# Final rows of an MLA / RG-LRU trunk normalised in place, with half of each row squared and weighted one product ahead, and one operand of the last projection split on VectorE

## Chip, cores and metric

The kernel runs on one core of one Trainium2 chip. The metric is the device time of one execution in microseconds (us); several executions are timed and their median is taken. One further execution is recorded by the hardware profiler, and every time of an instruction below is from that one.

## What is computed

A trunk of two layers, a latent-attention layer and an RG-LRU layer, over 1024 tokens and 16 leading meta tokens of width 1024, all in float32. The change lies in the end of the second layer and in the final norm:

```python
def rmsnorm(x, g):
    xf = x.astype(jnp.float32)
    y = xf * lax.rsqrt(jnp.mean(xf * xf, axis=-1, keepdims=True) + RMS_EPS)
    return (y * g.astype(jnp.float32)).astype(x.dtype)

# rglru_mixer: ... hs from the recurrence, gate from the input projection
    y = hs.astype(h.dtype) * jax.nn.silu(gate)
    return y @ w_out                       # (1040 x 1024) @ (1024 x 1024)

# after the two layers, h being the residual stream
    h = h + rglru_mixer(...)
    h = rmsnorm(h, final_norm_g)
    return h[:, N_META:]                   # the 1024 real tokens
```

## The kernel before

**Precision.** A float32 operand is split into a high part (a copy rounded to the matmul's type, `hi_of` at L80, ScalarE) and a low part (operand minus high part, `lo_of` at L83, VectorE). A product is three matmuls (`mm3`, L85 to L88: high x high, high x low, low x high), all accumulated in one PSUM bank.

**The last projection.** `Y` holds the gated mixer output, channels on partitions: `Y[:, ct, token]` for eight channel tiles `ct`. The projection of the 1024 real tokens is done as a 2 x 2 block scheme with seven block products of 512 x 512 x 512 in place of eight. `yq(cq, tq)` (L888) is a view of one block of `Y`; `a11, a12, a21, a22` (L974) are its four blocks, and sums and differences of them are made in place (L976, L993, L1007, L1008). The weight blocks and their sums come through `w_raw` / `w_load` (L864 to L874; a load with `add` accumulates by DMA on the GpSimd queue) and are split by `w_split` (L876) into buffers of the pools `wpg` and `pw1`, two of a kind. The operand from `Y` is split by `y_split` (L892): ScalarE copies (L893), VectorE subtracts (L894). `yc` (L935) does so for a whole block of 2048 elements a partition, into the tags `ych` and `ycl` of the pool `bo`, two buffers each. That pool opens at L926, when the pools of the layer's normalised input (`x2`) are closed: its buffers lie where that input lay, so they come free when the last gate product has read it.

**Products.** `product` (L896) runs four banks of 128 tokens, 12 matmuls of 512 columns in each. In program order the products are w1 (into banks `b2`), w7 (onto `b2`), w2 (into `b1`), w6 (onto `b2`), w5 (into `b3`), w3 (onto `b3`), w4 (onto `b2`). Between them `upd` (L946) adds or subtracts a bank into a half (`LEFT` or `RIGHT`, 512 columns) of a row tile `hr[i]`, 128 tokens x 1024, which was loaded from `hscr` at L932; a bank that a later product accumulates onto must have been read first. `hr[0..3]` are the first 512 tokens, `hr[4..7]` the last. The left half of `hr[0..3]` is final after w2's update, the right half of `hr[4..7]` after w3 begins, the right half of `hr[0..3]` after w3, the left half of `hr[4..7]` after w4.

**The final norm.** `square(i, half)` (L955) squares a half on ScalarE with its sum accumulated; the squares are thrown into an output tile `ot`, of which there are two (L958). `finish(i)` (L963) adds the two sums, takes a square root on ScalarE (L132) and refines it with four one-column VectorE instructions (L133 to L140), then writes `ot = hr * r * g_f` in two halves on VectorE (L970), each sent out by the SP queue (L971). `hr[0..3]` are finished after w3, `hr[4..7]` after w4.

**Order of the work.** The kernel is written on a tile framework that is told to plan with a timeline (L1084): when it is compiled, a planner with its own costs merges the program's instructions into one fixed order per engine, the earlier in the program the sooner among what it takes to be ready. On the chip each engine's queue is worked off in that order, and each instruction waits for its own operands. The ScalarE splits of the first operand `y1` (L913 to L918) already go into buffers of the recurrence (pool `bw`, tags `up`, `uh`, `ul`), ahead of the last gate product `b_gate(KT - 1, g7)`; the second operand, `y7` (L977, the block difference `a21 - a11`), goes through `yc`.

Of the kernel before, what the change touches and what calls it, by code (L numbers as in the profile page):

```python
# [8 lines left out]
F32 = mybir.dt.float32  # L9
# [8 lines left out]
P = 128  # L18
# [44 lines left out]
def trunk(ctx, tc, x, meta, a_norm_g, a_w_in, a_q_g, a_kv_g, a_w_uq, a_w_ukv, a_w_out,  # L63
# [832 lines left out]
    def product(banks, w, ys, first):  # L896
        for i in range(TI):
# [10 lines left out]
    w_load(ra, 0, 1)  # L908
    b_gate(KT - 1, g7)
# [3 lines left out]
    y1 = []  # L913
    for j in range(2):
        yh = pbw.tile([P, 4, 256], F32R, name=f"y1h{j}", tag=("up", "uh")[j], bufs=2)
        yl = pbw.tile([P, 4, 256], F32R, name=f"y1l{j}", tag=("up", "ul")[j], bufs=2)
        y_split(yq(0, 0, 256 * j, 256), yh, yl, -1)
        y1.append((yh, yl))  # L918
    w_load(ra, 1, 1, True)
    b2 = [ps_m(f"b2_{i}") for i in range(TI)]  # L920
    product(b2, w1, lambda i: (*y1[i // 2], (i % 2) * P), True)
    st_bw.close()
# [4 lines left out]
    st_fo, pfo = open_pool("fo", bufs=2, side="right")  # L927
# [25 lines left out]
    fms, junks = {}, {}  # L953

    def square(i, half):  # L955
        if i not in fms:
            fms[i] = sml.tile([P, 2], F32, name=f"fms{i}", tag="ms2", bufs=2 * TI)
            junks[i] = pfo.tile([P, D], F32, name=f"ot{i}", tag="ot", bufs=2)  # L958
        c = slice(half * 512, half * 512 + 512)
        nc.scalar.activation(junks[i][:, c], hr[i][:, c], AF.Square, scale=1.0 / 32.0,  # L960
                             accum_out=fms[i][:, half:half + 1])

    def finish(i):  # L963
        ot = junks[i]
        mt = sml.tile([P, 1], F32, name=f"fmt{i}", tag="ms")
        nc.vector.tensor_tensor(mt, fms[i][:, 0:1], fms[i][:, 1:2], ALU.add)
        r, _ = rms_r(mt, P, 1, f"f{i}")
        for half in range(2):
            c = slice(half * 512, (half + 1) * 512)
            nc.vector.scalar_tensor_tensor(ot[:, c], hr[i][:, c], r, g_f[:, c], ALU.mult, ALU.mult)  # L970
            nc.sync.dma_start(out[i * P:(i + 1) * P, c], ot[:, c])  # L971


    a11, a12, a21, a22 = yq(0, 0), yq(1, 0), yq(0, 1), yq(1, 1)  # L974
    w7 = w_split(ra, wpg, "wt3")
    nc.vector.tensor_tensor(a21, a21, a11, ALU.subtract)  # L976
    y7 = yc(a21, "s3")  # L977
# [110 lines left out]
```

## Time and profile before

| | us |
|---|---|
| median of 3 runs | 932.37 (928.75, 932.37, 932.37) |
| the profiled execution | 928.06 |
| its span, first to last instruction | 926.3 |
| TensorE busy in it | 888.9 (96%) |
| VectorE busy | 584.7 (63%) |
| ScalarE busy | 466.3 (50%) |

The profiled execution is a single one and lies just below the fastest of the three timed ones. The span leaves out the 1.8 us that lie around the first and last instruction. Mean granted TensorE clock is 0.994 of full speed (2.4 GHz). Engine names: PE is TensorE's matmul, PEld its weight load, DVE VectorE, ACT ScalarE, POOL GpSimd, SP the queue that issues most DMAs (SPq). Times of single instructions are from the start of the span.

### The profile page before, as it was taken

To read this page: it belongs to the slowest core of one execution; us is meant where nothing else is said; L and a number is where in the kernel's file an instruction comes from. 1 tells how busy PE (TensorE), PEld (TensorE's weight loads), DVE (VectorE), ACT (ScalarE), POOL (GpSimd) and SP (SyncE) were. 2 spreads that over 40 slices of the span, in tenths; PEclk is the share of its full clock that TensorE was granted. 3 is DMA by queue.
4 is the path that set the end of the run, shared out by engine and by line. 5 is a ranking of instruction groups with operands and counts; after the bars stand their busy time and mean duration, and the time that the engine had idled before them with its cause. 6 is when DMAs were issued, how large, how long until landed. Compare 5 with 4: busy or idle time off the path is not lost.

```text
span 926.3 us, 13669 instructions
## 1 busy us (share of the span) xinstructions
PE 888.9 (96%) x5279; PEld 816.0 (88%) x5279; DVE 584.7 (63%) x1206; ACT 466.3 (50%) x932; POOL 43.6 (5%) x46
## 2 busy tenths in 40 slices
PE   7999999999999999999999999999999999998993
PEld 5999999999999999999987778799989899886882
DVE  6666424416777677677675258764663947849986
ACT  6554322225664665665655146435648455582433
POOL 3000000000000000000000000000110201203100
PEclk9999999999999999999999999999999999999997
DMA  7123245221110010010032353241111111537613
GB/s 271 47 67 82 80 112 156 71 79 31 37 35 17 16 62 16 17 62 16 8 108 75 127 161 105 82 81 46 45 47 46 46 46 46 139 90 235 128 46 136
DMA packets 71169, 72.25 MB, mean 78 GB/s; under 512 B 15056, under 2 KB 52688, under 8 KB 71104
## 3 DMA queue, kind: packets, MB, share of 16 engines
q1 hardware_dynamic: 68928, 67.19, 23.4%
q0 software_dynamic: 2176, 4.19, 2.7%
q8 instruction: 41, 0.67, 0.3%
q14 instruction: 24, 0.20, 0.1%
HBM read 58.65 MB, written 12.71 MB: 77 GB/s over the span
## 4 chain that ended last, share of the span: by engine, by line
PE 89%; DVE 4%; ACT 3%; DMA 3%; issue 1%; SPq 1%; DVEq 0%; ACTq 0%
PE pt L536 4%; PE pu L88 3%; PE ga L86 3%; PE pu L86 3%; PE ga L87 3%; PE ga L88 3%; PE pu L87 3%; PE pg L87 3%; PE pg L88 3%; PE pg L86 3%; PE ao L86 3%; PE ao L88 3%; PE ao L87 3%; PE s L491 2%; PE o L88 2%; PE o L87 2%
## 5 line engine op out<-in xcount | busy, mean ns | idle before, releaser
L509 ACT ACTIVATE p<-s,m 116x116 f32<-116x116 f32 (+4 forms) x80 | 55.3, 693 | 42.8 <-PE pt L536 15.2
L80 ACT ACTIVATE pth<-pt 116x348 fp32r<-116x348 f32 (+5 forms) x152 | 57.5, 396 | 29.3 <-PE pt L536 25.7
L83 DVE TENSOR_TENSOR ptl<-pt,pth 116x348 fp32r<-116x348 f32 (+5 forms) x152 | 64.0, 437 | 10.3 <-ACT pth L80 9.6
L88 PE MATMUL pu<-x2h,l_wu 128*128 128x348 f32 (+1 forms) x192 | 61.5, 321 | 0.4 <-DVE l_wu L83 0.4
L88 PE MATMUL ga<-xth,l_wg 128*128 128x348 f32 (+1 forms) x192 | 61.7, 321 | 0.0
L87 PE MATMUL pu<-x2l,h_wu 128*128 128x348 f32 (+1 forms) x192 | 61.7, 321 | 0.0
L86 PE MATMUL pu<-x2h,h_wu 128*128 128x348 f32 (+1 forms) x192 | 61.7, 322 | 0.0
L87 PE MATMUL ga<-xtl,h_wg 128*128 128x348 f32 (+1 forms) x192 | 61.6, 321 | 0.0
L86 PE MATMUL ga<-xth,h_wg 128*128 128x348 f32 (+1 forms) x192 | 61.6, 321 | 0.0
L501 DVE CUSTOM_DVE_ANT_0 s<-s,maskt 116x116 f32<-116x116 f32 (+8 forms) x72 | 49.4, 686 | 17.6 <-PE s L495 17.6
L536 PE MATMUL pt<-ident,p 116*116 116x116 f32 (+1 forms) x360 | 54.5, 263 | 2.3 <-DVE ptl L83 1.8
L86 PE MATMUL ao<-wah,yh_a 128*128 128x512 f32 x128 | 50.5, 396 | 1.6 <-ACT yh_a L80 1.0
L87 PE MATMUL pg<-x2l,h_wbg 128*128 128x512 f32 x128 | 50.6, 396 | 0.0
L88 PE MATMUL pg<-x2h,l_wbg 128*128 128x512 f32 x128 | 50.3, 393 | 0.0
L88 PE MATMUL ao<-wah,yl_a 128*128 128x512 f32 x128 | 50.3, 394 | 0.0
L86 PE MATMUL pg<-x2h,h_wbg 128*128 128x512 f32 x128 | 50.2, 393 | 0.0
L87 PE MATMUL ao<-wal,yh_a 128*128 128x512 f32 x128 | 49.9, 391 | 0.0
L491 PE MATMUL s<-kh,qh 128*116 128x348 f32 (+7 forms) x120 | 42.1, 351 | 6.7 <-ACT p L509 6.7
L536 PEld LDWEIGHTS pt<-ident,p 116*116 116x116 f32 (+1 forms) x360 | 41.4, 135 | 6.0 <-DVE ptl L83 2.5
L87 PE MATMUL o<-ptl,v 116*128 116x348 f32 (+1 forms) x144 | 45.1, 313 | 0.0
L88 PE MATMUL o<-pth,v 116*128 116x348 f32 (+1 forms) x144 | 43.9, 305 | 0.0
L86 PE MATMUL o<-pth,v 116*128 116x348 f32 (+1 forms) x144 | 43.0, 298 | 0.0
(316 smaller groups left out, 2645.0 us busy)
## 6 DMA issues: line engine op xcount, KB each, us to landing
wg<-in_a_w_in SPq DMA_DIRECT2D x8, 512.0 KB, 3.9
wa<-in_a_w_out SPq DMA_DIRECT2D x8, 512.0 KB, 3.5
wu<-in_b_w_in SPq DMA_DIRECT2D x8, 512.0 KB, 4.0
wbg<-in_b_w_in SPq DMA_DIRECT2D x8, 512.0 KB, 4.0
hr<-hscr SPq DMA_DIRECT2D x8, 512.0 KB, 7.2
out_h<-ot SPq DMA_DIRECT2D x16, 256.0 KB, 2.1
x<-in_x SPq DMA_DIRECT2D x7, 512.0 KB, 3.3
wq<-in_b_w_out SPq DMA_DIRECT2D x6, 512.0 KB, 3.5
```

The costliest lines, as they stand in the source:

```text
L80: nc.scalar.activation(dst, src, AF.Copy)
L83: nc.vector.tensor_tensor(dst, src, bc(hi), ALU.subtract)
L86: nc.tensor.matmul(ps, lh, rh, start=start, stop=False, **kw)
L87: nc.tensor.matmul(ps, lh, rl, start=False, stop=False, **kw)
L88: nc.tensor.matmul(ps, ll, rh, start=False, stop=stop, **kw)
L491: nc.tensor.matmul(ps, a, kth[:, k0:k0 + w], start=True, stop=False)
L501: MKD[h, t] = nc.vector.tensor_tensor_reduce(pv, pv, mk, 1.0, -NEG, ALU.add, ALU.min, m[:, s:s + 1])
L509: MK[h, t] = nc.scalar.activation(dst, pv, AF.Exp, bias=mx, scale=-1.0, accum_out=l[:, s:s + 1])
L536: nc.tensor.transpose(pv[:nk, j], p[:, k0:k0 + nk], ident[:n, :n])
```

## The change

Three things change, all behind the last layer's input projection.

1. `y7` is split before the last gate product, by VectorE alone (`tensor_copy`, then `lo_of`), in two halves of 1024 elements, into buffers of the recurrence's pool `bw` (`uh`, `ul` and the two `uc`); `bw` is closed only after product w7, and the pool `fo` with `g_f` opens after that. The subtraction `a21 - a11` stands earlier in the program.
2. The updates stand later in the program: each set now follows the split of the operand that the next product needs, or the product after it.
3. The output tile `ot` is gone. `early` squares the half that is final first (its sum kept in `msa`, with the epsilon added); `early_g` multiplies that half by `g_f` in place; `late` squares the other half, takes the root of the sum of both, scales the early half on ScalarE in place (Copy with scale `r`) and does the late half on VectorE in place, each half sent out at once. The last bank of w4 is computed as two column halves of 256, and the last row's update and square follow in two parts.

```diff
     def product(banks, w, ys, first):
-        for i in range(TI):
+        for i in range(len(banks)):
...
     w_load(ra, 0, 1)
+    a11, a12, a21, a22 = yq(0, 0), yq(1, 0), yq(0, 1), yq(1, 1)
+    nc.vector.tensor_tensor(a21, a21, a11, ALU.subtract)
+
+    def y_pair(name, yv, sign, tags, by_dve=False):
+        pair = []
+        for j in range(2):
+            yh = pbw.tile([P, 4, 256], F32R, name=f"{name}h{j}", tag=tags[j][0], bufs=2)
+            yl = pbw.tile([P, 4, 256], F32R, name=f"{name}l{j}", tag=tags[j][1], bufs=2)
+            v = yv[:, :, 256 * j:256 * j + 256]
+            if by_dve:
+                nc.vector.tensor_copy(yh, v)
+                lo_of(yl, v, yh)
+            else:
+                y_split(v, yh, yl, sign)
+            pair.append((yh, yl))
+        return lambda i: (*pair[i // 2], (i % 2) * P)
+
+    y1 = y_pair("y1", a11, -1, (("up", "up"), ("uh", "ul")))
+    y7 = y_pair("y7", a21, 1, (("uh", "ul"), ("uc", "uc")), True)
     b_gate(KT - 1, g7)
...
-    product(b2, w1, lambda i: (*y1[i // 2], (i % 2) * P), True)
-    st_bw.close()
+    product(b2, w1, y1, True)
...
-    st_fo, pfo = open_pool("fo", bufs=2, side="right")
...
+    msa = [sml.tile([P, 1], F32, name=f"msa{i}", tag="msa", bufs=2 * TI) for i in range(2 * TI)]
+
+    def square(i, c, acc):
+        junk = pfo.tile([P, 512], F32, name=f"junk{i}_{c.start}", tag="junk", bufs=2)[:, :c.stop - c.start]
+        nc.scalar.activation(junk, hr[i][:, c], AF.Square, scale=1.0 / 32.0, accum_out=acc)
+
+    def early(i, c):
+        square(i, c, msa[i])
+        nc.vector.tensor_scalar(msa[i], msa[i], EPS, None, ALU.add)
+
+    def early_g(i, c):
+        nc.vector.tensor_tensor(hr[i][:, c], hr[i][:, c], g_f[:, c], ALU.mult)
+
+    def late(i, c, done):
+        ms = sml.tile([P, 1], F32, name=f"msb{i}", tag="msb", bufs=2)
+        square(i, c, ms)
+        ...
+        nc.scalar.activation(t, ms, AF.Sqrt, bias=msa[i])
+        nc.vector.tensor_scalar(v, ms, msa[i], -0.5, ALU.add, ALU.mult)
+        nc.vector.reciprocal(t, t)
+        nc.vector.scalar_tensor_tensor(r, t, v, t, ALU.mult, ALU.mult)
+        nc.vector.scalar_tensor_tensor(r, r, 1.5, t, ALU.add, ALU.mult)
+        rows = out[i * P:(i + 1) * P]
+        nc.scalar.activation(hr[i][:, done], hr[i][:, done], AF.Copy, scale=r)
+        nc.sync.dma_start(rows[:, done], hr[i][:, done])
+        left = LEFT if c.start < 512 else RIGHT
+        nc.vector.scalar_tensor_tensor(hr[i][:, left], hr[i][:, left], r, g_f[:, left], ALU.mult, ALU.mult)
+        nc.sync.dma_start(rows[:, left], hr[i][:, left])
...
     w7 = w_split(ra, wpg, "wt3")
-    nc.vector.tensor_tensor(a21, a21, a11, ALU.subtract)
-    y7 = yc(a21, "s3")
...
     product(b2, w7, y7, False)
+    st_bw.close()
+    st_fo, pfo = open_pool("fo", bufs=2, side="right")
     g_f = pfo.tile([P, D], F32, name="g_f", bufs=1)
...
     y2 = yc(a12, "a12")
-    for i in range(TI):
-        upd(b2[i], i, RIGHT, ALU.subtract)
-    nc.vector.tensor_tensor(a21, a22, a21, ALU.subtract)
...
     product(b1, w2, y2, True)
+    nc.vector.tensor_tensor(a21, a22, a21, ALU.subtract)
     w6 = w_split(ra, wpg, "wt2")
     y6 = yc(a21, "s2")
+    for i in range(TI):
+        upd(b2[i], i, RIGHT, ALU.subtract)
...
-    for i in range(TI):
-        upd(b1[i], i, LEFT, ALU.add)
-        square(i, 0) if i < 2 else None
...
     y5 = yc(a11, "s1")
+    for i in range(TI):
+        upd(b1[i], i, LEFT, ALU.add)
     nc.vector.tensor_tensor(a12, a12, a21, ALU.subtract)
...
     product(b3, w5, y5, True)
     w3 = w_split(r3, wpg, "wq22")
     y3 = yc(a12, "s4")
+    # the eight updates of b2 (RIGHT of hr[i] and hr[i + TI]) now stand here, after w5
+    for i in range(TI):
+        early(i, LEFT)
...
     y4 = yc(a22, "a22", -1)
     for i in range(TI):
+        early(i + TI, RIGHT)
+        early_g(i, LEFT)
+    for i in range(TI):
         upd(b3[i], i, RIGHT, ALU.add)
-        if i >= 2:
-            square(i, 0)
-        square(i, 1)
-        finish(i)
-    product(b2, w4, y4, False)
-    for i in range(TI):
-        square(i + TI, 1)
+        late(i, RIGHT, LEFT)
+        early_g(i + TI, RIGHT)
+    product(b2[:3], w4, y4, False)
+    cuts = [(b2[3][:, c:c + 256], slice(c, c + 256)) for c in (0, 256)]
+    for bank, c in cuts:
+        yh, yl, o = y4(3)
+        for k in range(4):
+            mm3(bank, yh[:, k, o:o + P], yl[:, k, o:o + P], w4[0][k // 2][:, k % 2, c], w4[1][k // 2][:, k % 2, c],
+                False, k == 3, skip_group_check=True)
+    for i in range(TI - 1):
         upd(b2[i], i + TI, LEFT, ALU.subtract)
-        square(i + TI, 0)
-        finish(i + TI)
+        late(i + TI, LEFT, RIGHT)
+    i = 2 * TI - 1
+    for j, (bank, c) in enumerate(cuts):
+        upd(bank, i, c, ALU.subtract)
+        if j == 0:
+            ms = sml.tile([P, 1], F32, name="msc", tag="msb", bufs=2)
+            square(i, c, ms)
+            nc.vector.tensor_tensor(msa[i], msa[i], ms, ALU.add)
+        else:
+            late(i, c, RIGHT)
```

## Rows read from the trace of the kernel before

**Rows 1.** Page, busy time by engine: us, share of the span, instructions.

```profile
PE 888.9 (96%) x5279; PEld 816.0 (88%) x5279; DVE 584.7 (63%) x1206; ACT 466.3 (50%) x932; POOL 43.6 (5%) x46
```

**Rows 2.** Busy us by stretch (length first): PE, PEld, DVE, ACT, POOL, clock, DMA.

```profile
840.60:851.30 10.70, 8.77 (x37) 6.58 (x36) 10.70 (x12) 2.98 (x2) 0.00 (x0) 1.00 0.66 188
851.30:862.30 11.00, 10.47 (x46) 8.20 (x45) 11.00 (x9) 3.93 (x3) 2.39 (x2) 1.00 0.76 167
862.30:874.00 11.70, 11.70 (x53) 9.63 (x52) 11.70 (x11) 5.15 (x7) 2.39 (x2) 1.00 0.63 117
874.00:888.00 14.00, 14.00 (x62) 11.35 (x61) 11.26 (x16) 4.99 (x4) 0.00 (x0) 1.00 0.16 55
888.00:899.00 11.00, 11.00 (x51) 9.07 (x50) 8.85 (x18) 6.08 (x9) 0.00 (x0) 1.00 0.00 1
899.00:910.40 11.40, 11.34 (x49) 8.80 (x47) 8.66 (x24) 3.75 (x12) 0.00 (x0) 1.00 0.47 174
910.40:926.30 15.90, 0.00 (x0) 0.00 (x0) 9.39 (x29) 5.81 (x20) 0.00 (x0) 0.66 0.38 139
```

**Rows 3.** Timeline of TensorE: start, us, instruction, [idle before <- releaser].

```profile
842.32 0.50 PE L88 MATMUL b<-h_wt,ycl_s 128*128 128x512 f32 x1 [1.12 <-DVE ycl_s L894]
...
845.74 0.50 PE L86 MATMUL b<-h_wt,ych_s 128*128 128x512 f32 x1 [0.81 <-DVE hr L949]
...
856.61 0.51 PE L88 MATMUL b<-h_wq,ycl_a 128*128 128x512 f32 x1 [0.53 <-DVE ycl_a L894]
...
909.94 0.40 PE L88 MATMUL b<-h_wt,ycl_a 128*128 128x512 f32 x1
```

**Rows 4.** Chain of waits, its end: start us, us, what.

```profile
914.57 2.02 DMA out_h<-ot
...
916.70 1.34 ACT ot L960 x4
```

**Rows 5.** Timelines of VectorE and ScalarE in the last rows' norm.

```profile
910.37 0.69 DVE L951 TENSOR_TENSOR hr<-hr,b 128x512 f32<-128x512 f32 x1 [0.68 <-PE b L88]
...
920.75 0.30 ACT L132 ACTIVATE t_f<-fmt,eps 128x1 f32<-128x1 f32 x1 [0.82 <-DVE fmt L966]
...
921.73 1.41 DVE L970 SCALAR_TENSOR_TENSOR ot<-hr,r_f,g_f 128x512 f32<-128x512 f32 x2
```

**Rows 6.** Timeline of VectorE, last gate product to w2.

```profile
821.36 1.23 DVE L809 TENSOR_TENSOR z<-z,uc 128x1040 f32<-128x1040 f32 x1
828.56 2.40 DVE L810 SCALAR_TENSOR_TENSOR z<-a,z 128x1040 f32<-128x1040 f32 x2 [5.96 <-ACT z L308]
...
839.43 2.84 DVE L894 SCALAR_TENSOR_TENSOR ycl_s<-Y,ych_s 128x2048 fp32r<-128x2048 f32 x1
842.19 2.31 DVE L813 TENSOR_TENSOR_SCAN z<-a,z 128x1040 f32<-128x1040 f32 x1
...
854.27 2.28 DVE L894 SCALAR_TENSOR_TENSOR ycl_a<-Y,ych_a 128x2048 fp32r<-128x2048 f32 x1
```

**Rows 7.** Groups by form: busy us, mean ns of one, idle before them.

```profile
L83 DVE TENSOR_TENSOR v<-pv,v 116x256 fp32r<-116x256 f32 x32 | 13.5, 421 | 2.0 <-ACT v L80 1.5
...
L517 DVE TENSOR_SCALAR p<-p,l 116x696 f32<-116x696 f32 x8 | 4.6, 579 | 0.1
...
L267 ACT ACTIVATE lt<-pk 128x256 f32<-128x256 f32 x8 | 3.0, 378 | 0.0
```

**Rows 8.** Timelines of GpSimd and of VectorE: multiplications beside a scan.

```profile
777.98 4.38 POOL L822 TENSOR_TENSOR Y<-Y,z 128x512 f32<-128x512 f32 x2 [32.03 <-DVE z L813]
...
836.67 3.45 POOL L822 TENSOR_TENSOR Y<-Y,z 128x512 f32<-128x512 f32 x2 [0.82 <-DVE z L813]
...
781.13 3.41 DVE L813 TENSOR_TENSOR_SCAN z<-a,z 128x1040 f32<-128x1040 f32 x1
```

**Rows 9.** Timeline of TensorE: two matmuls of 256 columns, start to start.

```profile
211.84 0.28 PE L86 MATMUL pv<-h_wkv,klh 128*116 128x256 f32 x1
211.96 0.28 PE L87 MATMUL pv<-l_wkv,klh 128*116 128x256 f32 x1
```

More of the change, by code (lines that the diff above doesn't have):

```diff
@@ L911, in trunk @@
     settle()
[L913 to L918, printed above, removed]
     w_load(ra, 1, 1, True)
     b2 = [ps_m(f"b2_{i}") for i in range(TI)]
-    product(b2, w1, lambda i: (*y1[i // 2], (i % 2) * P), True)
-    st_bw.close()
+    product(b2, w1, y1, True)
     st_bc.close()
@@ L951, in upd @@
             nc.vector.tensor_tensor(h_, h_, bank, ALU.subtract)
[L953 to L974, printed above, removed]
+    msa = [sml.tile([P, 1], F32, name=f"msa{i}", tag="msa", bufs=2 * TI) for i in range(2 * TI)]
@@ new lines, in square @@
+    def square(i, c, acc):
[9 more added lines that the diff above has]
+        square(i, c, ms)
+        v = sml.tile([P, 1], F32, name=f"v_f{i}", tag="rv")
+        r = sml.tile([P, 1], F32, name=f"r_f{i}", tag="rr")
+        t = sml.tile([P, 1], F32, name=f"t_f{i}", tag="rt")
+        nc.scalar.activation(t, ms, AF.Sqrt, bias=msa[i])
[9 more added lines that the diff above has]
+        nc.sync.dma_start(rows[:, left], hr[i][:, left])
@@ L997, in trunk @@
     product(b1, w2, y2, True)
+    nc.vector.tensor_tensor(a21, a22, a21, ALU.subtract)
     w6 = w_split(ra, wpg, "wt2")
     y6 = yc(a21, "s2")
+    for i in range(TI):
+        upd(b2[i], i, RIGHT, ALU.subtract)
     w_load(r5, 0, 1, True)
     w_load(ra, 1, 0, True)
-    for i in range(TI):
-        upd(b1[i], i, LEFT, ALU.add)
-        square(i, 0) if i < 2 else None
     nc.vector.tensor_tensor(a11, a11, a21, ALU.subtract)
-    nc.vector.tensor_tensor(a12, a12, a21, ALU.subtract)
     product(b2, w6, y6, False)
@@ L1013, in trunk @@
     y5 = yc(a11, "s1")
+    for i in range(TI):
+        upd(b1[i], i, LEFT, ALU.add)
+    nc.vector.tensor_tensor(a12, a12, a21, ALU.subtract)
     r3 = w_raw("wq22")
     w_load(r3, 1, 1)
-    for i in range(TI):
-        upd(b2[i], i, RIGHT, ALU.add)
-        upd(b2[i], i + TI, RIGHT, ALU.add)
     b3 = other("b3")
@@ L1024, in trunk @@
     y3 = yc(a12, "s4")
+    for i in range(TI):
+        upd(b2[i], i, RIGHT, ALU.add)
+        upd(b2[i], i + TI, RIGHT, ALU.add)
+    for i in range(TI):
+        early(i, LEFT)
     for i in range(TI):
@@ L1032, in trunk @@
     for i in range(TI):
+        early(i + TI, RIGHT)
+        early_g(i, LEFT)
+    for i in range(TI):
         upd(b3[i], i, RIGHT, ALU.add)
-        if i >= 2:
-            square(i, 0)
-        square(i, 1)
-        finish(i)
-    product(b2, w4, y4, False)
-    for i in range(TI):
-        square(i + TI, 1)
-        upd(b2[i], i + TI, LEFT, ALU.subtract)
-        square(i + TI, 0)
-        finish(i + TI)
+        late(i, RIGHT, LEFT)
[8 more added lines that the diff above has]
+    for i in range(TI - 1):
+        upd(b2[i], i + TI, LEFT, ALU.subtract)
+        late(i + TI, LEFT, RIGHT)
[8 more added lines that the diff above has]
+            late(i, c, RIGHT)
     st_fo.close()
```

## The prediction

> **What bounds the kernel now.** I read the page first: TensorE is busy for 96% of the span [rows 1], so over most of the program only what TensorE waits for can be won. The table of busy time by stretch then shows the exception [rows 2]: in the last stretch, 910.4 to 926.3, TensorE does nothing at all, and VectorE and ScalarE are busy for only 9.39 and 5.81 of 15.9 us. The stretches ahead of it, from 840.6 on, show something else: VectorE is busy without a gap up to 874 (10.70 of 10.70, 11.00 of 11.00, 11.70 of 11.70). So there are two places: a tail, and a passage where VectorE holds TensorE up.
>
> The timeline of TensorE gives the second [rows 3]: from w1 to w4 it is idle three times, 1.12 us for `ycl_s` (the low part of `y7`), 0.81 us for an update of `hr`, 0.53 us for `ycl_a` (the low part of `y2`), in sum 2.46 us; from 856.61 on it runs without a gap to its last matmul, which ends at 909.94 + 0.40 = 910.34. The tail is 926.3 - 910.34 = 15.96 us. The chain of waits shows what it is made of [rows 4]: the square of row tile 6 starts at 916.70, when the output transfer of an earlier row tile, begun at 914.57, has landed: there are two tiles `ot`, and the squares write into them. Only then come two squares (1.34 us), the root, and the two multiplications of the last row, 1.41 us from 921.73 on [rows 5]; 926.3 - 923.14 = 3.16 us more are the last transfer and the end of the program.
>
> **The tail after the change.** Squares go into a scratch tile that only ScalarE touches and rows are scaled in place, so no instruction waits for an output transfer any more. What then stands between the last matmul and the end, from the last row's work:
> - two updates of 256 columns, one after the other: VectorE's subtraction from PSUM at 256 columns took 0.42 us [rows 7]: 0.84 us;
> - the second square: a ScalarE square of 256 columns took 0.38 us [rows 7], and two of 512 with the readings of their sums 1.34 us [rows 4], so 0.38 to 0.67: 0.5 us; the first lies beside the second update;
> - from the start of the root to the start of the multiplication: 921.73 - 920.75 = 0.98 us [rows 5]. The extra additions (`msa`) lie ahead of it, beside the squares;
> - one half multiplied on VectorE, 1.41 / 2 = 0.70 us; the other half is a ScalarE copy beside it, at 1.34 / 2 = 0.67 us not longer;
> - 3.16 us as before.
>
> That is 6.2 us. Row tile 6, whose bank is done a quarter of w4 (2.8 us) earlier, needs 0.69 + 0.67 + 0.98 + 0.70 = 3.0 us, so its last multiplication can stand just ahead of the first update in VectorE's queue: between 0 and 0.70 us, I take 0.4. **Tail 6.6 us, 9.4 us less.**
>
> The last bank's 24 matmuls of 256 columns cost TensorE nothing: such matmuls start 0.12 us apart [rows 9], and 24 x 0.12 is the 2.8 us that a bank takes now. Whether the first half's update can run beside the second half's matmuls, no row shows: every read of a bank `b` here begins after that bank's last matmul, as the update at 910.37 does, 0.03 us after the end [rows 3, 5]. With overlap the first update and the first square's start leave the tail, 0.5 us; without it, nothing is won. I take nothing. The Trainium skill speaks against the split here: its page "PSUM — Partial Sum Buffer", section "PSUM bank collisions raise a hardware error", says that two engines may not touch one bank on the same partitions at the same time, not even at different columns. By that rule the tail stays at 6.6 us, against 6.1 us with overlap.
>
> **The passage at 840.** Removed from it: the ScalarE copy and the VectorE subtraction of `y7`, 2.84 us at 839.43 [rows 6], with a scan of the recurrence (842.19) queued behind it, behind that the update that TensorE waits for at 845.74, and further behind `ycl_a`. All three idle times are one queue. Added: four VectorE instructions of 1024 elements ahead of the last gate product's end. Their subtractions cost half of 2.28 us each; a copy from SBUF to SBUF isn't in the trace, and lies between the rate of the scaling at L517 (0.58 us for 696 elements [rows 7], so about 0.85) and that of a subtraction (1.14): together 4.0 to 4.6 us. VectorE is idle for 5.96 us before 828.56, after the last read of `uc` at 822.6 [rows 6], and `uh` and `ul` come free with the gate matmuls just before that: they fit, with 1.4 us to spare, and then cost nothing. If that cover is gone they go into the full passage (a rival below).
>
> What is late next? The scan moves up to where GpSimd multiplies (836.67 to 840.1). Beside such multiplications a scan took 3.41 us against 2.31, as `y7`'s subtraction took 2.84 against 2.28 [rows 6, 8]; so of 2.84 us between 1.7 and 2.8 are won. The update that TensorE resumes on at 845.74 then ends between 842.9 and 844.0, and TensorE, without the two idle times up to there, wants it at 845.74 - 0.81 - 1.12 = 843.8 [rows 3]: 0 to 0.2 us of idle time stay, I take 0.2. `ycl_a` is ready earlier by those 1.7 to 2.8 us and by one more instruction of 2048 elements, since the block subtraction (L993) is also moved behind it: at least 1.7 + 2.2 = 3.9 us, where 0.53 + 1.93 = 2.46 are needed; nothing stays there. **TensorE ends 2.46 - 0.2 = 2.3 us earlier, at 908.1.**
>
> **VectorE as the next bound.** The updates that are moved back, and the in-place weighting, are still to be done. Its busy time from 840.6 to the end is 71.56 us [rows 2]. After the change: minus 1.67 (the rest of `ycl_s` after 840.6), plus 0.5 for the slower scan and 0.3 for the split last update and one addition; eight of the sixteen multiplications at L970 (0.70) become plain ones in place at 0.69, the other eight stay: 70.7 us. From 840.6 to the end of its last multiplication (908.1 + 6.6 - 3.16 = 911.5) there are 70.9. So VectorE has 0.2 us to spare, while today it stands idle for 2.74 + 2.15 + 2.74 = 7.6 us in the three stretches before 910.4. The eight early weightings (5.5 us) and the updates moved back can fill these gaps, since nothing waits for them soon. If all are filled nothing is lost, if none 7.4 us; I take 1.2, near the filled end, because the work that fits is there. ScalarE gets eight copies (5.4 us) in stretches where it is busy for a half at most [rows 2]. SP's queue: the load of `g_f` now waits for w7's end and may hold the weight load queued behind it; what needs that load is w5, more than 20 us later.
>
> **Sum.** Span 926.3 - 9.4 - 2.3 + 1.2 = 915.8; execution 928.06 - 10.5 = 917.6. The profiled execution lies 4.3 us under the median of the three runs, which stand at two levels; the changed kernel's median may fall on either, so I add half, 2.1: **919.7 us**.
>
> **The rivals.** *VectorE runs out* (0.20): the planner's order leaves half or all of the gaps unfilled, and the last rows queue up: 2.5 to 6.2 us more, 922.2 to 925.9. For it speaks the sum of 70.7 against 70.9; against it that VectorE always finds work in rows 0 to 3 and the weightings. *TensorE's idle time stays* (0.13): the four new pieces are ordered behind 829, where VectorE is full; then at least the 2.3 us are lost and at most the 4.6 us as well: 922.0 to 926.6. *It doesn't do what it says* (0.07): the early half isn't early, and the four bottom rows' squares and weightings stand in the tail, 4 x (0.67 + 0.69) = 5.4 us more: 925.1, and up to no gain. *Slower* (0.05): ScalarE's queue between w3 and w4. A `late` copy waits for VectorE; if those of rows 0 to 3 are queued ahead of the splits that w4 needs, w4 starts only after w3's last bank plus 3.0 us for the row and at least 2 x 2.28 us for copying and subtracting `a22`: 7.6 us of idle TensorE. The clock then falls: in the last stretch, after TensorE stopped, the granted clock is 0.66 on the mean against 1.00 before [rows 2]; at 1.2 GHz w4's 11.4 us take up to 11.4 more: 927.3 to 938.7. It is slower than before from the point where stall and clock cost over 10.5 us together. Against it: the splits stand earlier in the program than `late`.
>
> **How the numbers follow.** The forecast as described has 0.55; its own range is 915.3 (gaps filled, no idle time left, column overlap, the lower level) to 922. The range that should hold 8 in 10 goes on to the top of the first two rivals: 915 to 926. A measurement of this kernel can tell about 0.5% (4.7 us) from no change, so faster is below 927.7: the forecast, nearly all of the first two rivals and half of the third make 0.89; the rest of them 0.06 for the same; the last rival 0.05 for slower.
>
> **What would show it.** Right: no wait of a ScalarE square for an output transfer; 6 to 7 us from the last matmul to the end; four 1024-element VectorE instructions between 818 and 829; no idle time of over 1 us between w1 and w2. Wrong: VectorE full after TensorE's end with more than one row left (first rival), idle time before w7 or w2 (second), before w4 (last). The first update of the last bank before the bank's last matmul would show the overlap.

## The result, and the profile after

The changed kernel takes 918.07 us, the median of four runs (916.80, 916.97, 919.16, 920.09), against 930.57 us (928.75 to 932.37) for the kernel before in the same comparison: a ratio of 0.9868, with an interval from 0.9833 to 0.9902. The forecast was 919.7 us in a range from 915 to 926.

The profiled execution of the changed kernel is the slowest of its four, 920.09 us, with a span of 918.3. It is best read by two landmarks, the start of w1's first matmul and the end of the last matmul, for what lies ahead of w1's start varies from run to run by more than the parts of the change are worth (last section).

| | before | after | difference |
|---|---|---|---|
| start of w1's first matmul | 829.41 | 833.22 | +3.8 |
| passage: w1's start to the end of the last matmul | 80.93 | 77.71 | -3.2 |
| tail: end of the last matmul to the end of the span | 15.96 | 7.37 | -8.6 |

The two lower lines are the change: 11.8 us. The two fastest runs of either kernel, 928.75 and 928.77 against 916.80 and 916.97, differ by 11.9.

The table of busy time by stretch, of after, in the columns of [rows 2]:

```profile
840.60:851.30 10.70, 10.62 (x46) 8.29 (x46) 10.70 (x12) 3.93 (x3) 3.39 (x2) 1.00 0.77 226
851.30:862.30 11.00, 11.00 (x50) 8.98 (x49) 11.00 (x9) 4.05 (x3) 1.19 (x1) 1.00 0.47 120
874.00:888.00 14.00, 14.00 (x63) 11.51 (x62) 14.00 (x20) 5.38 (x9) 0.00 (x0) 1.00 0.31 92
888.00:899.00 11.00, 11.00 (x50) 9.04 (x49) 11.00 (x21) 8.26 (x14) 0.00 (x0) 1.00 0.01 1
899.00:911.00 12.00, 11.93 (x64) 10.10 (x62) 10.17 (x35) 8.94 (x24) 0.00 (x0) 1.00 0.60 222
911.00:918.30 7.30, 0.00 (x0) 0.00 (x0) 3.25 (x11) 2.43 (x7) 0.00 (x0) 0.84 0.56 209
```

TensorE, at 8.77 of 10.70 us before, is now busy for 10.62 of them and throughout behind them; the list of what it waits for between 820 and 915 is empty. One small hold is in no list: the second bank's first matmul of w7 starts 0.49 us after the one ahead of it (846.92 and 847.41), where 0.23 is usual, just as the update of 846.67 ends. VectorE, which had gaps from 874 on [rows 2], is full up to 899. The timeline of VectorE shows what takes the place of [rows 6]: the four pieces of `y7`, the stretched scan, the block subtraction L1020, `ycl_a`, and behind it the split of a weight block.

```profile
818.46 0.69 DVE L919 CAST y7h<-Y 128x1024 fp32r<-128x1024 f32 x1
822.31 0.69 DVE L919 CAST y7h<-Y 128x1024 fp32r<-128x1024 f32 x1 [3.15 <-PE pz L88]
824.08 1.22 DVE L83 TENSOR_TENSOR y7l<-Y,y7h 128x1024 fp32r<-128x1024 f32 x1
827.62 1.23 DVE L83 TENSOR_TENSOR y7l<-Y,y7h 128x1024 fp32r<-128x1024 f32 x1
...
843.27 2.90 DVE L813 TENSOR_TENSOR_SCAN z<-a,z 128x1040 f32<-128x1040 f32 x1
...
849.67 2.28 DVE L1020 TENSOR_TENSOR Y<-Y 128x2048 f32<-128x2048 f32 x1
...
854.21 2.28 DVE L894 SCALAR_TENSOR_TENSOR ycl_a<-Y,ych_a 128x2048 fp32r<-128x2048 f32 x1
856.40 1.22 DVE L83 TENSOR_TENSOR l_wq<-wq,h_wq 128x1024 fp32r<-128x1024 f32 x1
```

And the tail, from the timeline of all engines, in place of [rows 3], [rows 4] and [rows 5]:

```profile
910.65 0.28 PE L88 MATMUL b<-h_wt,ycl_a 128*128 128x256 f32 x1
910.96 0.75 DVE L962 TENSOR_TENSOR hr<-hr,b 128x256 f32<-128x256 f32 x2
911.83 0.40 ACT L970 ACTIVATE junk<-hr 128x256 f32<-128x256 f32 x1
912.22 0.75 DVE L994 SCALAR_TENSOR_TENSOR hr<-hr,r_f,g_f 128x512 f32<-128x512 f32 x1
912.23 0.71 ACT L991 ACTIVATE hr<-hr,r_f 128x512 f32<-128x512 f32 x1
912.85 0.28 ACT L985 ACTIVATE t_f<-msb,msa 128x1 f32<-128x1 f32 x1
913.81 0.72 ACT L991 ACTIVATE hr<-hr,r_f 128x512 f32<-128x512 f32 x1 [0.68 <-DVE r_f L989]
913.81 0.75 DVE L994 SCALAR_TENSOR_TENSOR hr<-hr,r_f,g_f 128x512 f32<-128x512 f32 x1
914.56 0.33 SPq L992 DMA_DIRECT2D out_h<-hr  x1
914.98 0.39 SPq L995 DMA_DIRECT2D out_h<-hr  x1
```

No ScalarE square waits for an output transfer any more. Two updates, the second square, a copy and a multiplication of row tile 6 (L991 and L994 at 912.2, side by side), the root, the last copy and multiplication, two transfers: that is the whole tail.

### The profile page after: what moved, and what is told of

The parts are those of the page before. It is cut to its first block, busy times and chain, and to the rows that moved or that the text cites. A ratio compares the mean times of both kernels' runs of the same rounds, so it can differ in the third digit from the quotient of the medians.

```text
span 918.3 us, 13697 instructions
## 1 busy us (share of the span) xinstructions
PE 891.8 (97%) x5291; PEld 820.6 (89%) x5291; DVE 584.9 (64%) x1211; ACT 469.4 (51%) x941; POOL 43.4 (5%) x46
## 4 chain that ended last, share of the span: by engine, by line
PE 92%; ACT 3%; DVE 2%; issue 1%; DMA 1%; SPq 0%; ACTq 0%; DVEq 0%
PE pt L536 4%; PE pu L88 3%; PE ga L86 3%; PE pu L86 3%; PE ga L87 3%; PE ga L88 3%; PE pu L87 3%; PE ao L86 3%; PE ao L88 3%; PE ao L87 3%; PE pg L87 3%; PE pg L88 3%; PE pg L86 3%; PE s L491 2%; PE b L86 2%; PE b L88 2%
```

## The experiments

Passage and tail are from one profile each; medians are of the runs beside runs of the kernel before on the same chip. Where an edit doesn't touch them, the two stretches repeat closely: passages of 77.65 to 77.72 us in eight kernels (after, e4, e5, e8 to e12) and of 80.93 and 80.96 in two (before, e3), tails of 7.37 to 7.43 in four (after, e6, e7, e12). So 0.1 us is no difference between two profiles, and 0.3 us is one; the medians of whole runs, with intervals of 2 to 6 us, can't tell such parts.

| kernel | passage | tail | sum | median (before beside it) | ratio, interval |
|---|---|---|---|---|---|
| before | 80.93 | 15.96 | 96.9 | | |
| after | 77.71 | 7.37 | 85.1 | 918.07 (930.57) | 0.9868, 0.9833 to 0.9902 |
| e1_y7_only | 78.12 | 15.92 | 94.0 | 926.83 (929.90) | 0.9968, 0.9957 to 0.9979 |
| e2_norm_only | 80.63 | 7.53 | 88.2 | 921.24 (929.90) | 0.9899, 0.9878 to 0.9921 |
| e3_eight_tiles | 80.96 | 9.21 | 90.2 | 922.65 (929.90) | 0.9925, 0.9907 to 0.9943 |
| e4_nocut | 77.65 | 7.47 | 85.1 | 918.31 (929.50) | 0.9879, 0.9859 to 0.9899 |
| e5_two_banks | 77.71 | 7.08 | 84.8 | 918.67 (929.50) | 0.9885, 0.9867 to 0.9903 |
| e6_dve_more4 | 79.24 | 7.43 | 86.7 | 921.29 (929.50) | 0.9906, 0.9884 to 0.9928 |
| e7_y7_scalar | 78.79 | 7.37 | 86.2 | 919.40 (929.50) | 0.9897, 0.9874 to 0.9919 |
| e8_last_issue | 77.70 | 7.59 | 85.3 | 917.38 (930.10) | 0.9862, 0.9843 to 0.9880 |
| e9_no_early_g | 77.71 | 8.90 | 86.6 | 919.62 (930.10) | 0.9890, 0.9868 to 0.9911 |
| e10_pool_tail | 77.72 | 7.31 | 85.0 | 920.00 (930.10) | 0.9884, 0.9866 to 0.9901 |
| e11_stagger | 77.72 | 6.72 | 84.4 | 918.19 (930.29) | 0.9869, 0.9850 to 0.9889 |
| e12_old_order | 77.72 | 7.40 | 85.1 | 919.11 (930.29) | 0.9876, 0.9857 to 0.9894 |

**The seventh operand alone, and the norm alone.** The kernel before with part 1 of the change alone (with it, `bw` is closed and `fo` opened behind w7, as in the change), and with part 3 alone. The lines that count in the first:

```diff
-    nc.vector.tensor_tensor(a21, a21, a11, ALU.subtract)
-    y7 = yc(a21, "s3")
...
+    nc.vector.tensor_tensor(a21, a21, a11, ALU.subtract)            # ahead of b_gate(KT - 1, g7)
+    y7 = y_pair("y7", a21, 1, (("uh", "ul"), ("uc", "uc")), True)   # ahead of b_gate(KT - 1, g7)
```

> The kernel before with one part of the change alone: y7 split on VectorE ahead of the last gate product, into the buffers uh, ul and uc; updates and final norm as before. Two stretches of the trace are read: from w1's first matmul to the last matmul (80.9 us before, 77.7 after the whole change) and from there to the end (16.0 before, 7.4 after). If y7's split is what freed TensorE: 77.7 to 78.5 and 16.0, so 2.4 to 3.2 us less in all (ratio 0.9965 to 0.9975). If it was the later place of the updates: 80.5 to 81 and 16.0, no gain. If part of the idle time comes back at w2, since the block subtraction L993 and an update still stand ahead of the low part of y2: 78.5 to 79.5.

> The kernel before with the final norm of the change alone (squares ahead, weighting in place, no output tile, last bank in column halves); y7 and the updates as before. If the parts are independent: 80.9 us from w1 to the last matmul, 7.4 behind it, 8.6 us less in all (ratio about 0.991). If VectorE, which still splits y7 in the full passage, runs out at the end: 8.5 to 11 us behind the last matmul. If the norm's early work pushes the splits of the last products back: more than 81.5 us from w1 to the last matmul.

Part 1 alone shortens the passage by 2.81 us and leaves the tail at 15.92; TensorE waits for nothing between w1 and the last matmul, and ScalarE still waits twice, 8.0 us in all, for output transfers. Part 3 alone takes 8.4 us off the tail, 0.3 off the passage, and keeps the three idle times of [rows 3], in the timeline of TensorE of e2_norm_only:

```profile
846.62 0.50 PE L88 MATMUL b<-h_wt,ycl_s 128*128 128x512 f32 x1 [1.19 <-DVE ycl_s L894]
850.04 0.50 PE L86 MATMUL b<-h_wt,ych_s 128*128 128x512 f32 x1 [0.85 <-DVE hr L949]
860.90 0.50 PE L88 MATMUL b<-h_wq,ycl_a 128*128 128x512 f32 x1 [0.53 <-DVE ycl_a L894]
```

Both runs fit their first case. The two parts are separate gains: 2.9 and 8.7 us on the sum, 11.6 of the 11.8 that the whole change brings.

**The wait for output tiles alone.** The kernel before with a tile for each of the eight rows, nothing else:

```diff
-            junks[i] = pfo.tile([P, D], F32, name=f"ot{i}", tag="ot", bufs=2)
+            junks[i] = pfo.tile([P, D], F32, name=f"ot{i}", tag="ot", bufs=2 * TI)
```

> The kernel before with one number changed: eight output tiles in place of two, so that no square waits for an output transfer; all the work of the norm is done where it was before. If the wait for the transfers made the tail: update 0.7, square 0.7, sum and root 1.2, two multiplications 1.4, transfer and end 3.2, in sum 7.2 us, and up to 8.6 with row tile 6's two multiplications ahead in VectorE's queue, in place of 16.0; 7.4 to 8.8 us less in all (ratio about 0.991). If it was the amount of work behind the last matmul: only the 3.4 us wait goes, tail 12.6.

This one number takes 6.75 of the 8.6 us off the tail. The tail of 9.21 us lies 0.6 over the range of the first case, 7.2 to 8.6, and far from the 12.6 of the second. What is left is VectorE's queue, in its timeline of e3_eight_tiles (the last matmul ended at 911.59):

```profile
911.19 1.42 DVE L970 SCALAR_TENSOR_TENSOR ot<-hr,r_f,g_f 128x512 f32<-128x512 f32 x2
912.52 0.68 DVE L951 TENSOR_TENSOR hr<-hr,b 128x512 f32<-128x512 f32 x1
...
916.26 1.41 DVE L970 SCALAR_TENSOR_TENSOR ot<-hr,r_f,g_f 128x512 f32<-128x512 f32 x2
```

The last bank's update starts 0.93 us late, behind two multiplications of an earlier row.

**Without the early weighting.** The changed kernel with both halves multiplied on VectorE at the end:

```diff
-        early_g(i, LEFT)
...
-        early_g(i + TI, RIGHT)
...
-        nc.scalar.activation(hr[i][:, done], hr[i][:, done], AF.Copy, scale=r)
+        nc.vector.scalar_tensor_tensor(hr[i][:, done], hr[i][:, done], r, g_f[:, done], ALU.mult, ALU.mult)
```

> The changed kernel without the early weighting: the early half is still squared a product ahead, in place and without output tiles, but both halves are multiplied by the root's inverse and by g on VectorE at the end, as before the change; ScalarE's copies are gone. VectorE's eight multiplications of 0.69 us become eight of 0.75, at other places. Theory (VectorE's own queue sets the tail, which is why taking the wait for output tiles away alone left 9.21 us): the extra multiplications of rows 6 and 7 stand behind the last matmul on VectorE, 0.75 to 1.5 us more, tail 8.1 to 8.9 us; the passage stays at 77.7, since the multiplications move into gaps or behind. Rival (the 1.8 us between 9.21 and 7.37 come from the early squares and the cut, not from the weighting): tail 7.2 to 7.6 us, even a little less, with no copy ahead of the last root.

The tail grows by 1.53 us to 8.90, the top of the first range; the rival is out. VectorE's timeline shows four multiplications of rows 5 and 6 behind the last matmul's end (910.40), two of them ahead of the addition that the last root (912.82) needs and two ahead of the root's refinement (913.96). The first line shows, too, what releases the first update:

```profile
910.44 0.42 DVE L962 TENSOR_TENSOR hr<-hr,b 128x256 f32<-128x256 f32 x1 [0.18 <-PE b L88]
...
911.25 0.75 DVE L991 SCALAR_TENSOR_TENSOR hr<-hr,r_f,g_f 128x512 f32<-128x512 f32 x1
911.91 0.75 DVE L994 SCALAR_TENSOR_TENSOR hr<-hr,r_f,g_f 128x512 f32<-128x512 f32 x1
912.57 0.15 DVE L1077 TENSOR_TENSOR msa<-msa,msc 128x1 f32<-128x1 f32 x1
912.64 0.75 DVE L991 SCALAR_TENSOR_TENSOR hr<-hr,r_f,g_f 128x512 f32<-128x512 f32 x1
913.30 0.75 DVE L994 SCALAR_TENSOR_TENSOR hr<-hr,r_f,g_f 128x512 f32<-128x512 f32 x1
...
914.73 0.75 DVE L991 SCALAR_TENSOR_TENSOR hr<-hr,r_f,g_f 128x512 f32<-128x512 f32 x1
915.40 0.74 DVE L994 SCALAR_TENSOR_TENSOR hr<-hr,r_f,g_f 128x512 f32<-128x512 f32 x1
```

So the 8.6 us are 6.75 for the wait, 1.53 for the early weighting, and 0.3 for everything else that is changed.

**The cut of the last bank, and two banks.** First whole again, `product(b2, w4, y4, False)` and one `late` for all four rows; then cut, with each half in a fresh bank of its own, so that what the old bank held is subtracted earlier, by one update more:

```diff
+    upd(b2[3], 2 * TI - 1, LEFT, ALU.subtract)
-    cuts = [(b2[3][:, c:c + 256], slice(c, c + 256)) for c in (0, 256)]
+    cuts = [(ps_t(f"cut{c}")[:, :256], slice(c, c + 256)) for c in (0, 256)]
...
-                False, k == 3, skip_group_check=True)
+                k == 0, k == 3, skip_group_check=True)
```

> The changed kernel with the last bank whole again: one update of 512 columns, one square of 512, then the root. The changed kernel's trace shows both of its updates after the last matmul, 0.75 us together, a first square hidden beside the second update, and a second square with its reading of 0.59 us, so the cut can only have saved part of a square. Theory (the halves give TensorE's end nothing to overlap, since the bank is read only after its last matmul; VectorE's 3.3 us of work after that end set the tail): the update takes 0.68 instead of 0.75, the square 0.63 + 0.19 instead of 0.59, the root waits for the square and no longer for a copy ahead of it: tail 7.4 to 7.8 us, passage 77.7 unchanged. Rival (the cut is worth an early start of the first half): tail 7.9 us or more, 0.5 us and more over the changed kernel's 7.37.

> The changed kernel, with the last row tile's two halves of 256 columns in two fresh PSUM banks; what the old bank held before is subtracted from the row earlier by one more VectorE update of 0.68 us. Theory (reading one bank beside matmuls into the same bank is what the first update waited for): the first update of 256 columns starts 1.0 to 1.4 us before the last matmul's end, only one update of 0.4 us is left behind it, and the tail falls from 7.37 to between 6.5 and 7.0 us. Rival 1 (VectorE's queue holds the update, not the bank): the first update still starts after the last matmul's end or within 0.1 us of it, and the tail is 7.4 us, or up to 0.7 more for the added update. Rival 2 (two matmul streams in other banks cost TensorE something): passage over 77.9 us, against 77.7.

The cut is worth 0.1 us at most (7.47 against 7.37), as the theory had it. With two banks the first update does start ahead of the last matmul, which begins at 911.44 in e5_two_banks, and the second (911.76) at its end:

```profile
910.65 0.41 DVE L962 TENSOR_TENSOR hr<-hr,cut 128x256 f32<-128x256 f32 x1
```

The tail falls by 0.29 us only, to 7.08 us, a little over the expected range. ScalarE's timeline shows where the rest stays: the root still stands behind a copy of row 6, as in the changed kernel.

```profile
912.69 0.71 ACT L991 ACTIVATE hr<-hr,r_f 128x512 f32<-128x512 f32 x1
913.30 0.28 ACT L985 ACTIVATE t_f<-msb,msa 128x1 f32<-128x1 f32 x1
```

**Four multiplications more on VectorE.** The changed kernel, and ahead of `product(b3, w3, y3, False)`:

```diff
+    extra = pfo.tile([P, 512], F32, name="extra", bufs=1)
+    for i in range(4):
+        nc.vector.tensor_tensor(extra, hr[i % TI][:, LEFT], g_f[:, LEFT], ALU.mult)
```

> The changed kernel with four more VectorE multiplications of 512 columns into a scratch tile, ahead of product w3: 4 x 0.69 = 2.8 us more on VectorE, not part of the result. The changed kernel's VectorE is busy in every us from 840.6 to 899 and has 1.8 us of gaps between 899 and 911. Theory (the gaps were filled and about 1.8 us are spare, so that VectorE is near the bound but not yet the bound): 1 to 2 us of the 2.8 appear at the end, nearly all in the tail, 8.4 to 9.4 us. Rival 1 (VectorE is the bound already): all 2.8 us appear, tail or passage together 87.9 us against 85.1. Rival 2 (the order was only padded with early work, and VectorE has room): under 0.3 us appear.

Of 2.8 us added (2.4 in a full queue, where such multiplications start 0.60 us apart), 1.6 appear: the size that the theory gave, but at another place. The tail is unchanged (7.43); TensorE waits ahead of w3 for an update of `hr`, as its timeline in e6_dve_more4 shows:

```profile
890.13 0.47 PE L86 MATMUL b<-h_wq,ych_s 128*128 128x512 f32 x1 [1.30 <-DVE hr L960]
```

So VectorE has about 1 us to spare ahead of w3 in the changed kernel (0.8 or 1.2 by the one count or the other), and the first thing to give way is a bank that a product must wait for, not the tail.

**The copies of y7 on ScalarE.** One word of the changed kernel, `by_dve`, left off:

```diff
-    y7 = y_pair("y7", a21, 1, (("uh", "ul"), ("uc", "uc")), True)
+    y7 = y_pair("y7", a21, 1, (("uh", "ul"), ("uc", "uc")))
```

> The changed kernel with the two copies of y7's high part on ScalarE again, two of 1024 elements (1.06 us each, as y1's), in the same place and the same buffers; VectorE keeps the subtractions. Theory (what counts is that y7 is split ahead of the last gate's end, where VectorE has room, while ScalarE's chain there, from the last reading of pz to the scan, is the one that VectorE's full stretch waits for): the second copy stands in that chain with 1.06 us, the scan comes 1.0 to 1.1 us later, and TensorE has 0.3 to 1.1 us of idle time again before w7 or w2: passage 78.0 to 78.8 us against 77.7. Rival (only the place in the order counts, the engine doesn't): passage 77.6 to 77.8 and the total within 0.2 us of the changed kernel.

The passage is 1.08 us longer, and one idle time of TensorE is back. Timelines of ScalarE and of TensorE in e7_y7_scalar:

```profile
824.94 1.04 ACT L893 ACTIVATE y7h<-Y 128x1024 fp32r<-128x1024 f32 x1
825.88 2.21 ACT L308 ACTIVATE z<-z,c 128x1040 f32<-128x1040 f32 x2
```

```profile
855.87 0.50 PE L88 MATMUL b<-h_wq,ycl_a 128*128 128x512 f32 x1 [1.00 <-DVE ycl_a L894]
```

The second copy stands in ScalarE's chain that leads from the last reading of `pz` (the PSUM tile of the recurrence's gates) to the scan. VectorE's instruction behind that chain (L810) starts 0.1 us after w1 in place of 0.8 us before it, and `ycl_a` ends 2.1 us later against w1's start. The engine counts, not only the place in the order.

**The updates at their old places.** The changed kernel with part 2 undone:

```diff
     y2 = yc(a12, "a12")
+    for i in range(TI):
+        upd(b2[i], i, RIGHT, ALU.subtract)
+    nc.vector.tensor_tensor(a21, a22, a21, ALU.subtract)
...
-    for i in range(TI):
-        upd(b2[i], i, RIGHT, ALU.subtract)
```

and so on for the updates of `b1` and of `b2`'s later use.

> The changed kernel with the updates and block subtractions back at their places of before, seventh operand and norm as changed. Theory (y7's split ahead of w1 brought TensorE its time; the later place of the updates brought little, since the planner orders by what it takes to be ready): passage 77.7 to 78.2 us as with the split alone, TensorE waits for nothing over 0.3 us between w1 and the last matmul, tail 7.3 to 8.0 us. Rival 1 (the order of the updates is what takes ycl_a's idle time away): a wait of 0.3 to 0.6 us for ycl_a comes back, passage 78.2 to 78.6. Rival 2 (the later updates fill VectorE's gaps, and without them VectorE runs out at the end): VectorE is idle for over 3 us between 840 and 899, and the tail is 9 us or more.

Nothing moves: passage 77.72, tail 7.40, no wait of TensorE, VectorE without a gap from 840.6 to 899. On VectorE the order from the scan to `ycl_a` is the same as in the changed kernel, with L1020's counterpart ahead of `ycl_a`. Both rivals are out; part 2 is worth nothing here.

**The last transfers.** The last row's scaled half issued by ScalarE's queue in place of SP's:

```diff
-        nc.sync.dma_start(rows[:, done], hr[i][:, done])
+        (nc.scalar if i == 2 * TI - 1 else nc.sync).dma_start(rows[:, done], hr[i][:, done])
```

> The changed kernel, with one transfer moved: the scaled half of the very last row is sent out by ScalarE's queue, behind its copy, and no longer by SP's. In the changed kernel's trace both halves are done at 914.5, SP issues one at 914.56 (0.33 us) and the other at 914.98 (0.39 us), and the end lies 3.74 us after the last multiplication's end instead of the 3.16 of before. Theory (the second issue stands behind the first on one queue): both are issued within 0.1 us of each other, the end comes 3.2 to 3.4 us after the last multiplication, tail 6.9 to 7.1 us instead of 7.37. Rival (the end is set by the transfer itself or by the closing of the program, not by the issue): 3.7 us and a tail of 7.3 to 7.5 us as before the edit.

The rival holds, if a little above its range: from the end of the last multiplication (911.54) to the end there are 3.96 us, not less than the 3.74 of the changed kernel. The table of stretches shows what fills them, by its last two columns, DMA share and GB/s moved. Before, where the last multiplication ended at 923.14:

```profile
923.10:923.70 0.60, 0.00 (x0) 0.00 (x0) 0.04 (x1) 0.00 (x0) 0.00 (x0) 0.50 0.61 229
923.70:924.30 0.60, 0.00 (x0) 0.00 (x0) 0.00 (x0) 0.00 (x0) 0.00 (x0) 0.50 1.04 379
924.30:924.90 0.60, 0.00 (x0) 0.00 (x0) 0.00 (x0) 0.00 (x0) 0.00 (x0) 0.50 0.72 266
```

After, where it ended at 914.56:

```profile
915.10:915.70 0.60, 0.00 (x0) 0.00 (x0) 0.00 (x0) 0.00 (x0) 0.00 (x0) 1.00 0.63 232
915.70:916.30 0.60, 0.00 (x0) 0.00 (x0) 0.00 (x0) 0.00 (x0) 0.00 (x0) 0.75 1.02 382
916.30:916.90 0.60, 0.00 (x0) 0.00 (x0) 0.00 (x0) 0.00 (x0) 0.00 (x0) 0.50 0.82 307
```

And in e8_last_issue (ended at 911.54):

```profile
912.70:913.30 0.60, 0.00 (x0) 0.00 (x0) 0.00 (x0) 0.00 (x0) 0.00 (x0) 0.68 1.02 386
913.30:913.90 0.60, 0.00 (x0) 0.00 (x0) 0.00 (x0) 0.00 (x0) 0.00 (x0) 0.50 0.84 307
```

The two halves of the last row, 2 x 256 KB, go out at some 380 GB/s in one burst of 1.4 to 1.5 us, with one queue or with two, before as after. What differs is where the burst stands. It begins 0.8 to 0.9 us after the first of the two halves is ready. Before, the first half was multiplied 0.7 us ahead of the second, and that delay lay under the second multiplication; now both are ready together, and it lies open. Counted from the readiness of the first half, the end comes after 3.82 us before (922.48), 3.79 in e3, 3.77 after (914.53), and 3.99 in e8 (911.51). e9 tests it: there the halves are multiplied one after the other again (914.73 and 915.40 above), and the end comes 3.82 us after the first and, as before, 3.16 us after the second.

The Trainium skill states in "DMA: Bandwidth & Descriptors", section "Issuing engines are not separate DMA queues", that issuing from several engines saves only the issuing sequencer's time. The run agrees: 7.59 us of tail with two queues, 7.37 with one.

**All of the tail's rest at once.** Two attempts at a better version, both with the two banks. The first puts the scaled halves of row tiles 5 and 6 on GpSimd (and the last issue on ScalarE), the second holds each row's copy behind the next row's root by letting its sum go into the column that the root has read:

```diff
+            nc.gpsimd.tensor_scalar(hr[i][:, done], hr[i][:, done], r, None, ALU.mult)   # e10: row tiles 5 and 6
...
+        nc.scalar.activation(hr[i][:, done], hr[i][:, done], AF.Copy, scale=r, accum_out=acc)   # e11: row tiles 4 to 6
```

> The changed kernel with the three small things in its tail taken away together: the last row tile's halves in two banks, the scaled halves of row tiles 5 and 6 on GpSimd in place of ScalarE (so that no copy stands ahead of a root), and the last row's scaled half sent out by ScalarE's queue. Theory (these are the 0.3, 0.6 and 0.4 us that the tail still holds, and VectorE's queue of about 2.7 us is what is left): the root follows the last square at once, the last multiplication ends 2.8 to 3.1 us after the last matmul, the end 3.3 us later: tail 6.0 to 6.5 us against 7.37, total 1 us less. Rival (GpSimd beside VectorE costs what it saves, as scans were stretched beside it): its multiplication of 512 columns takes over 2 us or VectorE's instructions beside it get 10% or more longer, and the tail is 7.0 us or more.

> The changed kernel with its last row tile's halves in two banks, and with the scaled copies of row tiles 4 to 6 held behind the next row's root on ScalarE (the copy's sum goes into the column that the root has read). In the runs before it, the DMA engines are full from the last row's first half to the end of its second (382 and 307 GB/s in 915.7 to 916.9 of the changed kernel), and moving an issue to another queue gained nothing. Theory (the end is set by what the last row still has to send, two halves of 256 KB at some 380 GB/s, 1.4 us, from the moment that both are ready, and by VectorE's chain up to there): the last multiplication ends 2.9 to 3.2 us after the last matmul, row 6's halves are sent before that, and the end comes 3.7 to 3.9 us after it as in the changed kernel: tail 6.6 to 7.1 us, total 0.3 to 0.8 us under the changed kernel. Rival (row 6's copy, now late, is sent together with row 7's halves): 4.2 us and more from the last multiplication to the end, tail 7.2 to 7.6 us, no gain.

With GpSimd the rival holds: the tail is 7.31 us. The last multiplication ends 2.92 us after the last matmul, as the theory had it, but the end comes 4.39 us behind it: GpSimd takes over 2 us for 512 columns, row 6's half is ready only at 911.20, beside the last row's two (911.28 and 911.31), and three halves are sent one after the other.

```profile
909.08 2.12 POOL L994 TENSOR_SCALAR hr<-hr,r_f 128x512 f32<-128x512 f32 x1 [0.24 <-DVE r_f L989]
```

With the copy in ScalarE's idle time behind the root (timeline of ScalarE in e11_stagger) the tail is 6.72 us, inside the expected range, 0.65 less than in the changed kernel and 0.36 less than with the two banks alone:

```profile
911.07 0.29 ACT L985 ACTIVATE t_f<-msb,msa 128x1 f32<-128x1 f32 x1
911.40 0.72 ACT L993 ACTIVATE hr<-hr,r_f 128x512 f32<-128x512 f32 x1
```

The sum of passage and tail is the lowest of all, 84.4 us; the median (918.19 us, ratio 0.9869) cannot tell 0.7 us from the changed kernel's.

## Why the prediction was right, step by step

**The forecast came out, from the two places that it named.** What its sum (span 915.8) and the profile (918.3) differ by is four terms: 3.8 us more ahead of w1, 0.9 less in the passage, 0.8 more in the tail, and 1.2 less for VectorE, together 2.5 us. The first has nothing to do with the change (last section). Of the other three one goes against two, so the gain, 11.8 us against 10.5, is off by 1.3 us and not by the 2.9 that they come to in size: that is luck.

**Tail: -9.4 predicted, -8.6 measured.** Of the steps, the two updates took 0.75 us (0.84), root to multiplication 0.96 (0.98), the multiplication 0.75 (0.70), the second square 0.62 from the updates' end to the reading of its sum (0.5). Two terms were mis-sized. "3.16 us as before" is 3.74: the step counted from the end of the last multiplication, while what stays the same, at 3.8 us, is counted from the first half's readiness (e8, e9). And row 6's part, 0.4, is 0.52, and it stands in two queues and not in VectorE's alone: the copy ahead of the root on ScalarE and the multiplication on VectorE, ahead of the root's refinement, end within 0.05 us of each other (912.94 and 912.97). That the wait for the two output tiles was nearly the whole of the tail's loss is shown by one number changed (e3, 6.75 us).

**No overlap within a bank.** Right: the first update starts at 910.96, 0.03 us after the last matmul's end, although its own columns were done 1.4 us earlier, 12 matmuls 0.12 apart. In e9, where VectorE stood idle just before, the profile names a matmul as what released the first update, 0.04 us after the last matmul's end, and the second follows the first at once: so it is a wait in the program that holds both back. By the rule of the Trainium skill's page "PSUM — Partial Sum Buffer", section "PSUM bank collisions raise a hardware error", such a wait is needed; no run here tried without it. Halves in two banks do overlap (e5).

**Passage: -2.3 predicted, -3.2 measured.** The four pieces took 2 x 0.69 + 2 x 1.22 = 3.8 us, under the 4.0 to 4.6 worked out, all ahead of w1, so the cover held. The scan beside GpSimd took 2.90 us, within the 2.31 to 3.41 that the prediction allowed. `ycl_a` ended 23.3 us after w1's start against 27.1: 3.9 us sooner, the number predicted, but not by the way predicted. The block subtraction was to run behind `ycl_a`; it ran ahead of it (849.67 and 854.21), and e12 shows that its place in the program decides nothing. What ran behind it instead was one split of a weight block (856.40) and one update, which before ran ahead of `ycl_a`: that the sum is the same is luck.

The size was off for two reasons. The idle column understates what a stop of TensorE costs. From one matmul's start to the next, 1.51 us pass before 842.32 in place of 0.23, and 0.34 behind it, where the column has 1.12; the three stops of before add up in this way to 3.3 us and not 2.46. What stays in the changed kernel, the hold before 847.41, comes to 0.36 (0.2 predicted). In e6, 1.30 us of idle time make the passage 1.53 longer, in e7 1.00 make it 1.08. The rest, 0.3 us, comes with the norm: e2, with all three stops, has a passage of 80.63 us against 80.93, and e1, without the norm, 78.12 against 77.71; in e2 the matmuls of w4 start 0.229 us apart against 0.233 before. Why they do is open.

**VectorE as the next bound: +1.2 predicted, 0 measured.** All gaps up to 899 were filled, and about 1 us was still spare (e6). So the rival "VectorE runs out" was near: 2.8 us more work cost 1.6. The updates' later place has no part in it (e12). Of the other rivals none came: idle time is gone but for the 0.36 us, no row stands in the tail but 6 and 7, and TensorE doesn't wait ahead of w4. The rival that put the pieces where ScalarE or VectorE is full is seen in small in e7.

**The two levels.** Half of 4.3 us was added for them, from three runs. There are no two levels: 38 later runs of the kernel before lie between 928.25 and 932.40 us with no gap over 0.7. That the 930.2 us from which the forecast started fits the 930.57 of the comparison is luck. The bottom of the forecast's own range, 915.3, is not the sum of the four terms that it names either: 919.7 - 1.2 - 0.2 - 0.5 - 2.1 = 915.7.

## What to carry to other kernels

Look first for a buffer count in the last stretch: eight output tiles for two were 6.75 of the 11.8 us, and only then did the order of the last row's work matter. Treat the end of a kernel as work with its own bound: it came 3.8 us after the first of the last two halves was ready, so what counts there is how early the first half can be sent, and not only when the last one is done. Where a planner orders the queues, moving statements may change nothing (e12), while the engine that a piece runs on does (e7).

## What the runs showed of the hardware

**Falls of the clock move the start of w1.** In the profiled run of after TensorE is idle for 1.37 us before 47.23 (a transpose waits for ScalarE), as it is before 47.34 in the run of before; but in the first the granted clock then falls to half, the lower level, 1.2 GHz, for some 3 us, and in the second it doesn't. A stretch of after, then the same of before:

```profile
50.00:52.00 2.00, 2.00 (x9) 2.00 (x8) 2.00 (x5) 0.71 (x2) 0.00 (x0) 0.50 0.52 203
```

```profile
50.00:52.00 2.00, 2.00 (x14) 2.00 (x13) 2.00 (x5) 0.55 (x2) 0.00 (x0) 1.00 0.56 219
```

A second fall lies in 505 to 510 (0.66 on the mean against 1.00 in the run of before), behind a stretch in which TensorE was busy for 3.77 of 5.00 us, and before for 3.36. Each fall loses 1.7 us (an estimate: its length by the share of the clock that is missing in it), and the 14 profiles of this case line up by their number:

| falls ahead of w1 | kernels | w1's first matmul starts at |
|---|---|---|
| none | before, e1, e3, e4, e7, e8, e10 | 829.4 to 831.1 |
| one | e6 (in 550 to 570), e9, e11, e12 | 832.2 to 833.1 |
| two | after, e2, e5 | 833.2 to 834.0 |

So most of the 3.8 us by which w1 starts later in the profile of after are clock. The pieces of `y7` have no part in them: e2, which hasn't got them, has both falls, and the first matmul that reads the layer's normalised input `x2h` starts at 594.2 before and at 598.0 after, so all of the 3.8 us lie ahead of it, where the two programs are the same. What decides whether the clock falls is open.

**A copy on VectorE is not a subtraction.** On VectorE 1024 elements copied took 0.69 us and subtracted 1.22; copied on ScalarE they took 1.04 to 1.07. The Trainium skill's "VectorE: DVE Perf Modes", section "The perf-mode tier table (the rule you actually need)", has copies of float32 from SBUF at about twice the rate of an operation on two tensors. The trace agrees: the subtraction takes 1.8 times as long. The prediction had bounded the copy by a slower scaling from the trace, at 0.85.
